# Second half of a ConvFFN: split w_up pairs kept in DRAM, the down projection as seven products

## The chip, the cores and the metric

The kernel runs on one NeuronCore of a Trainium2 chip, in one launch. The time is device microseconds of that core. Engines: PE is TensorE (matmuls; PEld is its load of the stationary operand), DVE is VectorE, ACT is ScalarE, POOL is GpSimd, SP is SyncE, from whose queue nearly all DMAs of this stage are issued, in order.

## The reference

One decoder layer, sequence 2048, width 1024, d_ff 2816, all in float32. The change touches its last part:

```python
h2 = rmsnorm(x, norm2_g) * (1 + sc2) + sh2
u = causal_dwconv(h2 @ w_up, ffn_conv_w)      # three taps, 2 x 2816 columns
u_gate, u_val = jnp.split(u, 2, axis=-1)
y = (jax.nn.silu(u_gate) * u_val) @ w_down
return x + g2 * y
```

Ahead of it stand the conditioning vector's projections, an attention and a short convolution side by side, and the output projection; they are the same in both kernels.

## The kernel before

The FFN goes through the 2048 rows in two halves of 1024 (`hv` 0 and 1): `up(0)`, `down(0)`, `up(1)`, `down(1)`.

**Splitting.** No float32 matmul is done in one pass. An operand is split into a high part (ScalarE copies it to a narrower type) and a low part (VectorE subtracts the high part from the raw tile); a product is high x high + high x low + low x high, three matmuls. `up` splits into f16 (`high`, `low`), `down` into fp32r (`split_pair`).

**up.** There are 22 column pairs `i`: 128 columns of the gate with the 128 of the value that belong to them. A pair is a 2 x 2 block product (512 of the 1024 rows of w_up by 128 columns; two blocks of 512 sequence rows) done by Strassen's and Winograd's scheme: seven products of 4 x 3 = 12 matmuls in place of eight. The sums on the side of the sequence (`b11`, `t2`, ...) are made once a half and stay in SBUF. The sums on the side of the weights (`s1` to `s4`) are made in each half anew by `up_weights`: two loads of 512 KB (L1303), two scalings on ScalarE (L1309), four sums on VectorE (L1289, L1290), splits (L1207, L1210). This is a generator, and the steps for pair i+1 are called between the products of pair i. The pairs of split weights lie in tiles `wo..0` and `wo..1`, two sets by turns. The products are gathered from PSUM by ScalarE copies and VectorE sums; then come the convolution's taps (L1391, L1396), the silu (L1405), the product y (L1408) and its store to DRAM (`y_sc`, L1409). These last steps are the generator `finish`; those of pair i are called in the time of pair i+1, and those of the last pair in `down`.

**down.** Four products per half (row block of 512 by column half of 512), each of 22 steps of 12 matmuls into four accumulators (L142). For a step, `load_pair` loads 256 KB of y and 256 KB of w_down (L1348, L1349) into a tile `raw`; `split_pair` makes `hi` (L1354) and `lo` (L1355). Each of the tags raw, hi and lo has four buffers. Loads are called up to five steps ahead, splits two. The first three steps are loaded and split in the last pair of `up` (`first_pairs`). At the end of a product `add_gated` multiplies each accumulator by the gate (L1200), adds it to x1 (L1201) and writes it out. `side` is other work called between the steps: the last `finish`, and in `down(0)` norm2 of the second half's rows and `first_weights`, which makes the weights of the second half's first pair.

**Order.** `K` keeps an instruction in the order of the program on its engine; so the order of calls is the order on the engines. An engine that waits holds all that stands behind it; a DMA queue likewise.

Of the kernel before, what the change touches and what calls it, by code (L numbers as in the profile page):

```python
# [9 lines left out]
F32 = mybir.dt.float32  # L10
# [18 lines left out]
NT = S // P  # L29
KD = D // P  # L30
NPAIR = DFF // P
EPS = 1e-6
NEG = -1.0e38
LN_PS = 9.704060527839234
# [11 lines left out]
def kernel(  # L46
# [37 lines left out]
    m_at = [dram.tile([P, S], F32, name=f"m_at{i}") for i in range(4)]  # L84
    m_cv = [dram.tile([P, S], F32, name=f"m_cv{i}") for i in range(4)]
    x1_sc = [dram.tile([P, D], F32, name=f"x1_sc{i}") for i in range(NT)]
    y_sc = [dram.tile([P, S], F32, name=f"y_sc{i}") for i in range(NPAIR)]

    ident = const.tile([P, P], F32, name="ident")
    make_identity(nc, ident)  # L90
# [1095 lines left out]
    with ExitStack() as ph:  # L1186
# [107 lines left out]
        def up_pair():  # L1294
            n, j = divmod(used[0], 4)
            used[0] += 1
            return [fb.tile([P, 1024], F16, tag=f"wo{order[2 * j + e]}{n % 2}", name="pair") for e in range(2)]

        def up_weights(i):

            raws = [raw_tile() if i else fp.tile([P, 1024], F32, tag="first", name="raw", bufs=2) for _ in range(2)]
            for raw, ct in zip(raws, (i, NPAIR + i)):
                nc.sync.dma_start(  # L1303
                    raw.rearrange("p (k n) -> p k n", n=P), w_up[:, ct * P : (ct + 1) * P].rearrange("(k p) n -> p k n", p=P)
                )
# [24 lines left out]
            low(raws[1], *pc)  # L1330
            yield

        ready = {}

        def first_weights():

# [15 lines left out]
        def split_pair(raw):  # L1352
# [3 lines left out]
            y, wd = halves((hi, lo))  # L1356
            return (*y, *wd)

        raws, pairs = {}, {}

        def first_pairs(hv):

            for i in range(3):
                raws[4 * hv, i] = load_pair(4 * hv, i)
            yield
            for i in range(3):
                pairs[4 * hv, i] = split_pair(raws.pop((4 * hv, i)))
                yield
            while True:
                yield  # L1370

        def up(hv):
# [25 lines left out]
            def finish(i, p1, Y, gate, val, yg):  # L1398

                taps(yg, gate, i)  # L1400
                add(val[:, 2:514], p1, Y)
                yield
                yv = tap(val, NPAIR + i)
                keep_halo(val, NPAIR + i)
                K(A.activation(yg, yg, AF.Silu))  # L1405
                taps(yv, val, NPAIR + i)
                yield
                K(V.tensor_tensor(yv, yg, yv, op=ALU.mult))  # L1408
                nc.sync.dma_start(y_sc[i][:, hv * 1024 : (hv + 1) * 1024], yv)  # L1409
                yield  # L1410

            wts, ops = ready.pop("wts"), ready.pop("ops")
            last = None
# [47 lines left out]
        def down(hv, side):  # L1461

            todo = [(n, i) for n in range(4 * hv, 4 * hv + 4) for i in range(NPAIR)]
# [30 lines left out]
            for _ in side:  # L1494
                pass

        steps = {Q: norm2(Q) for Q in range(4)}
        weights = first_weights()
        early = chain(steps[0], (None for _ in range(1)), steps[1], weights)
# [36 lines left out]
```

## Time and profile before

| | |
|---|---|
| median of 3 runs | 2413.41 us (2413.23 to 2414.85) |
| the profiled execution | 2413.08 us, with a span of 2411.3 |
| granted TensorE clock | 0.997 |
| TensorE busy | 2328.6 us, 97% of the span |
| VectorE busy | 1804.9 us, 75% |
| ScalarE busy | 1304.2 us, 54% |
| start of down(0) | 1516.2 us |
| start of down(1) | 2166.95 us |
| last matmul | 2406.3 us |

The durations come from the profiled execution; its span runs from the first to the last instruction, and the device time is 1.8 us longer. A window row shows how long each engine was busy in that stretch of the span, the granted clock (1.00 is full) and the DMA load. A group row gives the count, the busy time and the mean of one instruction, and the idle time ahead of the group with what ended it.

### The profile page before, as it was taken

The page shows a single profiled execution, that of the slowest core. Times are in us where ns is not written, and L with a number is a line of the kernel's source. Part 1 is how long each engine was busy: PE and PEld are TensorE (multiplying, and loading weights), DVE is VectorE, ACT ScalarE, POOL GpSimd, SP SyncE. Part 2 cuts the span into 40 slices and gives each one's busy share as a digit, 9 for nine tenths or more (in the row PEclk, how much of TensorE's full clock was granted, in tenths as well). Part 3 has the DMA queues.
Part 4 walks back from the last instruction along what each step waited for, and adds up shares of the span by engine and source line. Part 5 has one row for each costly group of instructions (what it writes and reads, how often), then busy time and mean ns, then how long its engine had stood idle before and what let it go on. Part 6 is the DMA issues. An engine that isn't in the chain of part 4 may idle for free.

```text
span 2411.3 us, 38606 instructions
## 1 busy us (share of the span) xinstructions
PE 2328.6 (97%) x14472; PEld 1403.3 (58%) x14472; DVE 1804.9 (75%) x3430; ACT 1304.2 (54%) x2136; POOL 338.5 (14%) x282
## 2 busy tenths in 40 slices
PE   5899999999999898999999999999999999999999
PEld 5764554444677675444444444788854444448887
DVE  6768885553999897366888888667878888885554
ACT  5645544320888896344565565554545565554332
POOL 0211111101777872000000000000000000000000
PEclk9999999999999999999999999999999999999999
DMA  9356685522999996353222222677632222236775
GB/s 280 133 160 169 175 249 178 155 90 81 172 190 193 190 192 168 114 172 99 88 88 88 88 88 79 227 244 222 220 126 88 88 88 88 88 105 215 230 227 183
DMA packets 428708, 368.71 MB, mean 153 GB/s; under 512 B 184208, under 2 KB 327912, under 8 KB 427496
## 3 DMA queue, kind: packets, MB, share of 16 engines
q1 hardware_dynamic: 421400, 349.40, 51.8%
q10 hardware_dynamic: 4752, 8.46, 1.0%
q0 software_dynamic: 2368, 8.39, 0.9%
q8 instruction: 113, 1.85, 0.3%
q14 instruction: 75, 0.61, 0.1%
HBM read 267.54 MB, written 65.08 MB: 138 GB/s over the span
## 4 chain that ended last, share of the span: by engine, by line
PE 85%; DVE 7%; ACT 3%; issue 2%; DMA 2%; POOL 0%; SPq 0%; DVEq 0%; ACTq 0%; POOLq 0%
PE acc L1383 33%; PE acc L142 30%; PE pr L142 10%; PE pv L142 2%; PE pt L1064 2%; PE ps L1003 1%; PE ps L1004 1%; DVE near L1071 1%; PE po L1100 1%; DVE s_t L1027 1%; PE po L1102 1%; PE po L1101 1%; ACT s_t L1044 1%; DMA far<-wide 1%; DMA raw<-in_w_down_dram 1%
## 5 line engine op out<-in xcount | busy, mean ns | idle before, releaser
L1383 PEld LDWEIGHTS <-pair 128*128 128x128 f16 x3696 | 360.9, 98 | 436.8 <-issue 0.3
L1383 PE MATMUL acc<-t,pair 128*128 128x512 f16 x2112 | 477.4, 379 | 0.0
L1383 PE MATMUL acc<-b,pair 128*128 128x512 f16 x1584 | 363.5, 379 | 0.0
L1355 DVE TENSOR_TENSOR lo<-raw,hi 128x1024 fp32r<-128x1024 f32 x176 | 211.9, 1223 | 154.7 <-ACT hi L1354 154.2
L1354 ACT ACTIVATE hi<-raw 128x1024 fp32r<-128x1024 f32 x176 | 182.4, 1055 | 178.3 <-PE acc L142 141.8
L142 PE MATMUL acc<-hi 128*128 128x512 f32 x704 | 277.0, 393 | 1.6 <-DVE t L1200 1.6
L142 PE MATMUL acc<-lo,hi 128*128 128x512 f32 x704 | 274.6, 390 | 0.6 <-DVE lo L1355 0.5
L142 PE MATMUL acc<-hi,lo 128*128 128x512 f32 x704 | 274.5, 390 | 0.0
L1396 DVE SCALAR_TENSOR_TENSOR w<-w,fcw,w 128x1024 f32<-128x1024 f32 x176 | 226.1, 1285 | 34.6 <-ACT w L1391 25.5
L142 PEld LDWEIGHTS <-h 128*128 128x128 f16 x1344 | 130.1, 98 | 97.7 <-DVE h L355 5.4
L1207 ACT ACTIVATE pair<-raw 128x1024 f16<-128x1024 f32 x132 | 138.3, 1049 | 68.5 <-DVE raw L1290 68.4
L142 PE MATMUL acc<-wp,mp 128*128 128x512 f16 x768 | 170.6, 381 | 1.1 <-DVE raw L956 1.0
L1391 ACT ACTIVATE w<-w,fcw 128x1024 f32<-128x1024 f32 x88 | 100.7, 1144 | 130.9 <-DVE w L1289 130.9
L1044 ACT ACTIVATE s_t<-s_t,nb,cst 128x2048 f32<-128x2048 f32 (+15 forms) x128 | 164.7, 1288 | 4.8
L1210 DVE TENSOR_TENSOR pair<-raw,pair 128x1024 f16<-128x1024 f32 x132 | 160.8, 1218 | 4.7 <-ACT pair L1207 4.7
L142 PEld LDWEIGHTS acc<-hi 128*128 128x128 f32 x704 | 132.2, 188 | 31.1 <-DVE t L1200 4.4
L142 PEld LDWEIGHTS acc<-lo,hi 128*128 128x128 f32 x704 | 132.3, 188 | 28.3 <-DVE lo L1355 1.6
L142 PEld LDWEIGHTS acc<-hi,lo 128*128 128x128 f32 x704 | 132.2, 188 | 27.7
L1056 POOL TENSOR_TENSOR wide<-s_t,wide 128x1024 f16<-128x1024 f32 x64 | 136.7, 2136 | 5.3
L1027 DVE CUSTOM_DVE_ANT_0 s_t<-ps,nf,mx 128x512 f32<-128x512 f32 (+1 forms) x192 | 119.5, 643 | 17.7 <-PE ps L1006 9.4
L142 PEld LDWEIGHTS <-mp 128*128 128x128 f16 x768 | 75.1, 98 | 88.7 <-issue 2.9
L142 PE MATMUL pr<-h,wh 128*128 128x512 f16 x576 | 126.5, 379 | 0.0
(344 smaller groups left out, 4184.7 us busy)
## 6 DMA issues: line engine op xcount, KB each, us to landing
raw<-in_w_up_dram SPq DMA_DIRECT2D x88, 512.0 KB, 3.8
raw<-y_sc SPq DMA_DIRECT2D x176, 256.0 KB, 4.1
raw<-in_w_down_dram SPq DMA_DIRECT2D x176, 256.0 KB, 4.4
wx<-in_w_up_dram SPq DMA_DIRECT2D x88, 256.0 KB, 3.5
y_sc<-w SPq DMA_DIRECT2D x44, 512.0 KB, 2.6
wm<-in_w_ada_dram SPq DMA_DIRECT2D x128, 128.0 KB, 3.2
wr<-in_w_in_dram SPq DMA_DIRECT2D x40, 256.0 KB, 4.5
x_t<-in_x_dram SPq DMA_DIRECT2D x16, 512.0 KB, 5.3
```

The source lines that it names most:

```text
L142: ins = T.matmul(acc, lhsT=a, rhs=b, start=st, stop=sp)
L1027: K(V.tensor_tensor_reduce(out=s_t[:, o0 + c0 : o0 + c0 + cw], in0=ps[:, 0:cw], in1=nf[:, c0 : c0 + cw], scale=1.0, scalar=-3.0e38 if g == ...
L1044: K(A.activation(cols, cols, AF.Exp, bias=nb[:, p : p + 1], scale=qk[:, 4:5], accum_out=un["l"][:, p : p + 1]))
L1056: K(G.tensor_tensor(wide[:, 1, :], s_t[:, WB * P : WU], wide[:, 0, :], op=ALU.subtract))
L1064: K(T.transpose(pt[:, b * P : (b + 1) * P], s_t[:, (b0 + b) * P : (b0 + b + 1) * P], ident))
L1207: K(A.activation(hi, raw, AF.Copy))
L1210: K(V.tensor_tensor(lo, raw, hi, op=ALU.subtract))
L1354: K(A.activation(hi, raw, AF.Copy))
L1355: K(V.tensor_tensor(lo, raw, hi.bitcast(F32), op=ALU.subtract))
L1383: K(T.matmul(acc, lhsT=a, rhs=b, start=st, stop=sp, skip_group_check=True))
L1391: K(A.activation(y, u[:, 0:1024], AF.Copy, scale=fcw[:, ct : ct + 1]))
L1396: K(V.scalar_tensor_tensor(y, u[:, m : m + 1024], fcw[:, m * 44 + ct : m * 44 + ct + 1], y, op0=ALU.mult, op1=ALU.add))
```

## The change

In the first half `up` also stores the split weights of each pair (`keep_weights`: eight DMAs, 1.84 MB). In the second half they are read back by eight loads (`kept_weights`); there are no loads of w_up, scalings, sums or splits of it there. `kept_first` takes the place of `first_weights` in the first down.

`down(0)` stays (now `down_plain`). `down(1)` is `down_seven`: the rows of the second half's two blocks, the two column halves of w_down and the two halves of each of 11 pairs of d_ff tiles make 2 x 2 blocks again, and seven products of 11 steps do the work of four of 22. Its operands are made in `up(1)`: `down_inputs` stores the pieces of y and four sums of them (`t1` to `t4`), `down_weights` loads w_down, multiplies it by the gate, makes four sums and stores all of that. Most of these stores are put off (`store_later`) to the start of the next pair (`flush`). The gate being in the weights, an eviction is one addition (`evict`); one product is evicted by ScalarE copies, and 12 additions go to POOL. Products use two sets of four accumulators by turns.

```diff
-    y_sc = [dram.tile([P, S], F32, name=f"y_sc{i}") for i in range(NPAIR)]
+    y_sc = [dram.tile([P, S // 2], F32, name=f"y_sc{i}") for i in range(NPAIR)]
+    y_op = {n: [dram.tile([P, 512], F32, name=f"y_{n}_{j}") for j in range(NJ)] for n in ("b11", "b21", "b22", "t1", "t2", "t3", "t4")}
+    w_op = {n: [dram.tile([P, D], F32, name=f"w_{n}_{j}") for j in range(NJ)] for n in ("a11s3", "a12a22", "s1s2", "s4")}
+    up_sc = [dram.tile([P, 7 * D], F16, name=f"up_sc{i}") for i in range(NPAIR)]
...
-            pa, pb, pc, pd = [up_pair() for _ in range(4)]
+            pa, pb, pc, pd = made[i] = [up_pair() for _ in range(4)]
...
+        made = {}
+        def kept_columns(pairs):
+            at = 0
+            for both in pairs:
+                for t in both:
+                    n = 512 if both is pairs[3] else D
+                    yield t[:, 0:n], slice(at, at + n)
+                    at += n
+        def keep_weights(i):
+            for t, c in kept_columns(made.pop(i)):
+                K(nc.sync.dma_start(up_sc[i][:, c], t))
+        def kept_weights(i):
+            pairs = [up_pair() for _ in range(4)]
+            for t, c in kept_columns(pairs):
+                K(nc.sync.dma_start(t, up_sc[i][:, c]))
+            yield [*halves(pairs[0]), *halves(pairs[1]), *halves(pairs[2]), halves(pairs[3])[0]]
+            while True:
+                yield
...
+        def kept_first():
+            wts = kept_weights(0)
+            ready["ops"] = next(wts)
+            ready["wts"] = wts
+            yield
...
+        def load_operands(p, j):
+            w, y = plan[p]
+            n, e = place[w]
+            raw = raw_tile()
+            K(nc.sync.dma_start(raw[:, 0:512], y_op[y][j]))
+            K(nc.sync.dma_start(raw[:, 512:1024], w_op[n][j][:, e * 512 : (e + 1) * 512]))
+            return raw
...
+        stores, sums = [], {}
+        def store_later(dst, src):
+            stores.append(lambda: K(nc.sync.dma_start(dst, src)))
+        def flush():
+            while stores:
+                stores.pop(0)()
+        def down_inputs(i, y):
+            j = i // 2
+            a, b = y[:, 0:512], y[:, 512:1024]
+            if i % 2 == 0:
+                t12 = fq.tile([P, 1024], F32, tag="lo", name="t12", bufs=4)
+                K(nc.sync.dma_start(y_op["b11"][j], a))
+                sub(t12[:, 0:512], b, a)
+                store_later(y_op["t1"][j], t12[:, 0:512])
+                sums["t12"], sums["b"] = t12, b
+                return
+            t12, b12 = sums["t12"], sums["b"]
+            t34 = fq.tile([P, 1024], F32, tag="lo", name="t34", bufs=4)
+            K(nc.sync.dma_start(y_op["b21"][j], a))
+            K(nc.sync.dma_start(y_op["b22"][j], b))
+            sub(t12[:, 512:1024], b, t12[:, 0:512])
+            sub(t34[:, 0:512], b, b12)
+            sub(t34[:, 512:1024], a, t12[:, 512:1024])
+            store_later(y_op["t2"][j], t12[:, 512:1024])
+            store_later(y_op["t3"][j], t34[:, 0:512])
+            store_later(y_op["t4"][j], t34[:, 512:1024])
+        def down_weights(j):
+            wa, wb = [fp.tile([P, 1024], F32, tag="first", name="wd", bufs=2) for _ in range(2)]
+            for e, w in enumerate((wa, wb)):
+                K(nc.sync.dma_start(w, w_down[(2 * j + e) * P : (2 * j + e + 1) * P, :]))
+            yield
+            wc, wd = [fq.tile([P, 1024], F32, tag="lo", name="wd", bufs=4) for _ in range(2)]
+            a11, a21, a12, a22 = wa[:, 0:512], wa[:, 512:1024], wb[:, 0:512], wb[:, 512:1024]
+            s1, s2, s4 = wc[:, 0:512], wc[:, 512:1024], wd[:, 0:512]
+            for w in (wa, wb):
+                K(V.tensor_tensor(w, w, gates[:, D : 2 * D], op=ALU.mult))
+                yield
+            add(s1, a21, a22)
+            sub(a21, a11, a21)
+            yield
+            sub(s2, s1, a11)
+            sub(s4, a12, s2)
+            for n, w in (("a11s3", wa), ("a12a22", wb), ("s1s2", wc)):
+                store_later(w_op[n][j], w)
+            store_later(w_op["s4"][j][:, 0:512], s4)
             while True:
                 yield
...
-                K(V.tensor_tensor(yv, yg, yv, op=ALU.mult))
-                nc.sync.dma_start(y_sc[i][:, hv * 1024 : (hv + 1) * 1024], yv)
+                if hv == 0:
+                    K(V.tensor_tensor(yv, yg, yv, op=ALU.mult))
+                    nc.sync.dma_start(y_sc[i], yv)
+                else:
+                    y = fq.tile([P, 1024], F32, tag="hi", name="y", bufs=4)
+                    K(V.tensor_tensor(y, yg, yv, op=ALU.mult))
+                    down_inputs(i, y)
                 yield
...
+                flush()
...
                 product(X, o11, "b11", True)
-                wts = up_weights(i + 1) if i + 1 < NPAIR else first_pairs(hv)
+                if i + 1 < NPAIR:
+                    wts = (kept_weights if hv else up_weights)(i + 1)
+                else:
+                    wts = first_pairs(load_operands if hv else load_pair, hv)
                 ops = next(wts)
+                if hv and i % 2:
+                    next(wsum)
...
+                if hv == 0:
+                    keep_weights(i)
+                elif i % 2:
+                    next(wsum)
+                else:
+                    wsum = down_weights(i // 2)
+                    next(wsum)
                 product(Z, os1, "t1", True)
...
+                if hv and i % 2:
+                    next(wsum)
                 add(gate[:, 514:1026], u2, Z)
...
+                if hv and i % 2:
+                    next(wsum)
                 product(Y, o22, "t4", False)
...
+        def down_seven(side):
...
+            def x1_tiles(c, n):
+                xs[c, n] = [fb.tile([P, 512], F32, tag=f"wo{4 * c + t}1", name="xs") for t in range(4)]
+                for xp, r in zip(xs[c, n], rows[c]):
+                    K(nc.sync.dma_start(xp, x1_sc[r.start // P][:, n * 512 : (n + 1) * 512]))
...
+            def gadd(o, a, b):
+                K(G.tensor_tensor(o, a, b, op=ALU.add))
+            def evict(p, t):
+                a = acc[t]
+                if p == 0:
+                    K(A.activation(u2[t], a, AF.Copy))
+                elif p == 1:
+                    add(u2[t], u2[t], a)
+                elif p == 2:
...
+                elif p == 3:
+                    add(u3[t], u2[t], a)
+                    gadd(u3[t], u3[t], xs[1, 1][t])
...
+                else:
+                    c, n = ((0, 1), (1, 0))[p - 5]
+                    add(xs[c, n][t], xs[c, n][t], a)
+                    write(c, n, t, xs[c, n][t])
+            flush()
+            extra = {(2, 2): (0, 0), (2, 6): (1, 1), (4, 3): (0, 1), (5, 2): (1, 0)}
...
+                if (p, j) == (0, 4):
+                    flush()
+                if (p, j) in extra:
+                    x1_tiles(*extra[p, j])
+                if j == 6 and p in (4, 5):
+                    c, n = ((0, 1), (1, 0))[p - 4]
+                    for t in range(4):
+                        gadd(xs[c, n][t], xs[c, n][t], u2[t])
+                if j == 0:
+                    if p in (0, 4):
...
+                    acc = sets["b" if p in (1, 3, 5) else "a"]
+                if j != NJ - 2:
+                    for t in range(4):
+                        c = slice(t * P, (t + 1) * P)
+                        for jj in (j,) if j < NJ - 1 else (j - 1, j):
+                            yh, yl, wh, wl = pairs[p, jj]
+                            for a, b, st, sp in (
+                                (yh, wh, jj == 0 and p in (0, 1, 3, 4), False), (yh, wl, False, False), (yl, wh, False, jj == NJ - 1)
+                            ):
+                                K(T.matmul(acc[t], lhsT=a[:, c], rhs=b, start=st, stop=sp, skip_group_check=True))
+                        if j == NJ - 1:
+                            evict(p, t)
...
-        for hv in range(2):
-            last = up(hv)
-            down(hv, last if hv else chain(last, steps[2], steps[3], first_weights()))
+        down_plain(chain(up(0), steps[2], steps[3], kept_first()))
+        down_seven(up(1))
```

On SyncE, from the last y store of the first half into the first down (`up_sc` are the kept weights, `raw` the tile of a step of down), the rows before are

```order
L1409 DMA y_sc_115<-w_18033 128x1024
L1348 DMA raw<-y_sc_98 128x512
L1349 DMA raw<-in_w_down_dram 128x512
L1348 DMA raw<-y_sc_99 128x512
L1349 DMA raw<-in_w_down_dram 128x512
```

and now

```order
L1514 DMA y_sc_115<-w_18344 128x1024
L1351 DMA up_sc_259<-pair 128x1024 x6
L1351 DMA up_sc_259<-pair 128x512 x2
L1383 DMA raw<-y_sc_98 128x512
L1384 DMA raw<-in_w_down_dram 128x512
```

Eight stores have come in front of the load of step 3 (`y_sc_98` is its y).

On VectorE, in the last column pair of the second half and the start of the second down, the rows before are (L1355 is the low part of a step of down, `acc` a PSUM tile, L1396 a tap; the waits are named by engine or DMA semaphore)

```order
L1289 TENSOR_TENSOR t2_23300<-t2_23222,acc_23194 128x512 [waits PE_49]
L1289 TENSOR_TENSOR w4_23230<-t2_23300,t2_23286 128x512 [waits DVE_49,Activation_49]
L1289 TENSOR_TENSOR w4_23229<-t2_23245,acc_23195 128x512 [waits DMAHW0_49,PE_49]
L1396 SCALAR_TENSOR_TENSOR w4_23316<-w4_23229,fcw_133,w4_23316 128x1024 [waits Activation_49]
L1396 SCALAR_TENSOR_TENSOR w4_23316<-w4_23229,fcw_133,w4_23316 128x1024 [waits DVE_49]
L1289 TENSOR_TENSOR w4_23230<-t2_23222,acc_23194 128x512 [waits PE_49]
L1355 TENSOR_TENSOR lo_23359<-raw_23330,hi_23358 128x1024 [waits DMAHW1_49,DMAHW0_49,Activation_49]
```

and now (`wd_23503` and `wd_23504` are two tiles of w_down, gated by L1463; `wd_23593` and `wd_23594` hold their sums; L1390 is now the low part of a step of down, L1500 a tap)

```order
L1463 TENSOR_TENSOR wd_23504<-wd_23504,gates_283 128x1024
L1293 TENSOR_TENSOR t2_23678<-t2_23596,acc_23567 128x512 [waits PE_49]
L1293 TENSOR_TENSOR w4_23604<-t2_23678,t2_23664 128x512 [waits DVE_49,Activation_49]
L1293 TENSOR_TENSOR wd_23593<-wd_23503,wd_23504 128x512 [waits PE_49]
L1294 TENSOR_TENSOR wd_23503<-wd_23503 128x512 [waits DVE_49]
L1293 TENSOR_TENSOR w4_23603<-t2_23619,acc_23568 128x512
L1294 TENSOR_TENSOR wd_23593<-wd_23593,wd_23503 128x512
L1294 TENSOR_TENSOR wd_23594<-wd_23504,wd_23593 128x512 [waits DVE_49,PE_49]
L1500 SCALAR_TENSOR_TENSOR w4_23696<-w4_23603,fcw_276,w4_23696 128x1024 [waits Activation_49]
L1500 SCALAR_TENSOR_TENSOR w4_23696<-w4_23603,fcw_276,w4_23696 128x1024 [waits DVE_49]
L1293 TENSOR_TENSOR w4_23604<-t2_23596,acc_23567 128x512
L1390 TENSOR_TENSOR lo_23754<-raw_23725,hi_23753 128x1024 [waits DMAHW1_49,DMAHW2_49,PE_49,Activation_49]
```

The low parts of steps 0 to 2 (`lo_23622` to `lo_23648` in the change) stand ahead of the sums of w_down; the sum into `wd_23593` waits for TensorE to have read `lo_23622`, which is the low part of step 0, and the one into `wd_23594` for `lo_23644`, that of step 1. The low part of step 3 (`lo_23754`) stands behind them.

On SyncE, at the same place, before (`raw_23330` is step 3 of the second down):

```order
L1409 DMA y_sc20_115<-w4_23224 128x1024 [waits DMAHW7_49,DVE_49]
L1348 DMA raw_23330<-y_sc3_98 128x512 [waits DMAHW0_49,Activation_49]
L1349 DMA raw_23330<-in_w_down_dram 128x512 [waits DMAHW1_49]
L1348 DMA raw_23333<-y_sc4_99 128x512 [waits DMAHW2_49,Activation_49]
L1349 DMA raw_23333<-in_w_down_dram 128x512 [waits DMAHW3_49]
```

and now, with two stores of y ahead of these rows (`raw_23725` is step 3):

```order
L1425 DMA w_a11s3_10_204<-wd_23503 128x1024 [waits DMAHW5_49,DVE_49]
L1425 DMA w_a12a22_10_215<-wd_23504 128x1024 [waits DMAHW6_49]
L1425 DMA w_s1s2_10_226<-wd_23593 128x1024 [waits DMAHW7_49,DVE_49]
L1425 DMA w_s4_10_237<-wd_23594 128x512 [waits DMAHW0_49,DVE_49]
L1405 DMA raw_23725<-y_b11_3_120 128x512 [waits DMAHW1_49,Activation_49]
L1406 DMA raw_23725<-w_a11s3_3_197 128x512 [waits DMAHW2_49]
```

Step 3's loads stood behind one store, of y; now they stand behind six, four of them of the gated weights and their sums, which wait for VectorE.

More of the change, by code (lines that the diff above doesn't have):

```diff
@@ L31 @@
 NPAIR = DFF // P
+NJ = NPAIR // 2
 EPS = 1e-6
@@ L1357, in split_pair @@
             return (*y, *wd)
+        plan = (("a11", "b11"), ("s2", "t2"), ("a12", "b21"), ("s3", "t3"), ("s1", "t1"), ("a22", "t4"), ("s4", "b22"))
+        place = {
+            "a11": ("a11s3", 0), "s3": ("a11s3", 1), "a12": ("a12a22", 0), "a22": ("a12a22", 1), "s1": ("s1s2", 0), "s2": ("s1s2", 1),
+            "s4": ("s4", 0),
+        }
+        def load_operands(p, j):
[5 more added lines that the diff above has]
+            return raw
@@ L1359, with first_pairs @@
         raws, pairs = {}, {}
-        def first_pairs(hv):
+        def first_pairs(load, hv):
             for i in range(3):
-                raws[4 * hv, i] = load_pair(4 * hv, i)
+                raws[0, i] = load(0, i)
             yield
             for i in range(3):
-                pairs[4 * hv, i] = split_pair(raws.pop((4 * hv, i)))
+                pairs[0, i] = split_pair(raws.pop((0, i)))
                 yield
+            while True:
+                yield
+        stores, sums = [], {}
@@ new lines, in down_weights @@
+        def down_weights(j):
[11 more added lines that the diff above has]
+            sub(a21, a11, a21)
+            yield
+            sub(s2, s1, a11)
[3 more added lines that the diff above has]
+            store_later(w_op["s4"][j][:, 0:512], s4)
@@ L1407, in finish @@
                 yield
-                K(V.tensor_tensor(yv, yg, yv, op=ALU.mult))
-                nc.sync.dma_start(y_sc[i][:, hv * 1024 : (hv + 1) * 1024], yv)
+                if hv == 0:
[5 more added lines that the diff above has]
+                    down_inputs(i, y)
                 yield
             wts, ops = ready.pop("wts"), ready.pop("ops")
-            last = None
+            last = wsum = None
             for i in range(NPAIR):
                 o11, o12, os2, os4, os3, o22, os1 = ops
+                flush()
                 X, Y, Z = [
@@ L1459, in up, with down_plain @@
             return last
-        def down(hv, side):
-            todo = [(n, i) for n in range(4 * hv, 4 * hv + 4) for i in range(NPAIR)]
+        def down_plain(side):
+            todo = [(n, i) for n in range(4) for i in range(NPAIR)]
             loaded = split = 3
```

32 lines of the change are left out of this document (added).

## The prediction

> **What bounds the kernel now.** The page's head was read first: which engine fills the span, and what the chain that ended last is made of.
>
> ```profile
> span 2411.3 us, 38606 instructions
> PE 2328.6 (97%) x14472; PEld 1403.3 (58%) x14472; DVE 1804.9 (75%) x3430; ACT 1304.2 (54%) x2136; POOL 338.5 (14%) x282
> PE 85%; DVE 7%; ACT 3%; issue 2%; DMA 2%; POOL 0%; SPq 0%; DVEq 0%; ACTq 0%; POOLq 0%
> ```
>
> TensorE is the bound over the whole, but a share of the span says nothing about one stage. So the second view is the table of windows for the stages that the change touches: in order down of the first half, up of the second, down of the second, and ten dense microseconds near the start of the first down. Columns: window, its length, busy time of PE, PEld, DVE, ACT and POOL with instruction counts, granted clock, DMA share, GB/s.
>
> ```profile
> 1520.00:1765.00 245.00, 242.77 (x1091) 198.21 (x1090) 166.88 (x206) 129.59 (x155) 0.00 (x0) 1.00 0.72 232
> 1790.00:2160.00 370.00, 370.00 (x1716) 167.44 (x1714) 329.48 (x368) 216.79 (x287) 0.00 (x0) 1.00 0.27 86
> 2168.00:2404.00 236.00, 236.00 (x1042) 195.51 (x1042) 125.46 (x116) 90.68 (x86) 0.00 (x0) 1.00 0.68 215
> 1535.00:1545.00 10.00, 10.00 (x46) 8.29 (x45) 2.45 (x2) 7.26 (x12) 0.00 (x0) 1.00 0.89 320
> ```
>
> In the second half PE is busy 370.00 of 370.00 and 236.00 of 236.00. Two things follow: taking other engines' work out of the second up can gain nothing there, and each matmul taken out of the second down is gained whole, if the rest keeps up. The third view gives the price of a matmul. The timeline shows SyncE's loads, which in steady state are paced by the products that free the buffers (columns: start, duration, engine, line, operation, tiles, count).
>
> ```profile
> 1225.77 4.84 SPq L1303 DMA_DIRECT2D raw<-in_w_up_dram  x2
> 1298.29 4.85 SPq L1303 DMA_DIRECT2D raw<-in_w_up_dram  x2
> 2191.47 0.32 SPq L1348 DMA_DIRECT2D raw<-y_sc  x1
> 2213.23 0.32 SPq L1348 DMA_DIRECT2D raw<-y_sc  x1
> ```
>
> The first two rows stand four column pairs apart: 72.52/4 = 18.13 us for a pair's 84 matmuls. The others stand eight steps of down apart: 21.76/8 = 2.72 us for 12 matmuls, 0.2267 us each.
>
> **Part 1, fewer matmuls.** The second down has 4 x 22 steps of 12 now, 1056 matmuls; seven products of 11 steps have 924. 132 x 0.2267 = 29.9 us less, the 924 keeping their form. One step still loads 512 KB per 2.72 us, as before, so the 215 GB/s stay. Its VectorE work falls (an eviction is one sum, not a product and a sum), the twelve sums on POOL each have 10 steps before someone wants them, and products alternate between two sets of accumulators. Value **-29.9**; the cover is that load rate, and it is the rate of before.
>
> **Part 2, the tail.** After the last matmul two VectorE operations follow one another; one is left.
>
> ```profile
> 2406.30 0.39 PE L142 MATMUL acc<-hi,lo 128*128 128x512 f32 x1
> 2406.72 0.69 DVE L1200 TENSOR_TENSOR t<-acc,gates 128x512 f32<-128x512 f32 x1
> 2407.45 0.69 DVE L1201 TENSOR_TENSOR xs<-xs,t 128x512 f32<-128x512 f32 x1
> ```
>
> 2407.45 - 2406.72 = 0.7: value **-0.7**.
>
> **Part 3, inside the second up.** The groups of that stage (window 1785 to 2165; busy, mean ns):
>
> ```profile
> L1210 DVE TENSOR_TENSOR pair<-raw,pair 128x1024 f16<-128x1024 f32 x62 | 75.5, 1218 | 0.0
> L1290 DVE TENSOR_TENSOR raw<-raw 128x512 f32<-128x512 f32 x40 | 27.7, 692 | 1.4
> L1408 DVE TENSOR_TENSOR w<-w,w 128x1024 f32<-128x1024 f32 x21 | 25.6, 1219 | 0.0
> L1210 DVE TENSOR_TENSOR pair<-t,pair 128x512 f16<-128x512 f32 x20 | 13.7, 684 | 0.0
> ```
>
> Per column pair VectorE loses three wide lows (3.65), a narrow one (0.68) and four sums (4 x 0.69), 7.1 us. Per two pairs it gains two gate products (2 x 1.22) and eight sums (8 x 0.69), 4.0 us a pair. It was 89% busy (329.48 of 370) and goes to about 72%. ScalarE only loses work. TensorE was full and stays full: **0**. What hides the new work is the DMA. Per two pairs it now moves 3.67 MB of kept weights in, 1.05 MB of w_down in, 1.84 MB of sums of w_down out and 1.84 MB of y out, 8.39 MB in 36.26 us: 231 GB/s, against 86. The windows show 232 GB/s at a share of 0.72 and 320 at 0.89, both with mostly reads; here 44% are writes, which no row shows at that rate. Bounds: 0, and what rival B prices. In the first half the stores of split weights add 1.84 MB per 18.13 us, from 86 to about 190 GB/s; same answer, 0.
>
> **Part 4, the start of the second down.** This is the part that the diff doesn't tell. In the last column pair of up, the rows of VectorE show the sum into `wd_23593` behind a wait on TensorE that was not there before. The tiles of `down_weights` share four buffers with the low halves of the first products: that sum must wait until step 0 of the new down is through, `wd_23594` until step 1. On SyncE the stores of these tiles stand ahead of the load of step 3. Steps 0 to 2 are loaded early; step 3 is late. Its price is built from these rows (the third is from the list of the tile raw, 1480 to 1560):
>
> ```profile
> L1354 ACT ACTIVATE hi<-raw 128x1024 fp32r<-128x1024 f32 x176 | 182.4, 1055 | 178.3 <-PE acc L142 141.8
> L1355 DVE TENSOR_TENSOR lo<-raw,hi 128x1024 fp32r<-128x1024 f32 x176 | 211.9, 1223 | 154.7 <-ACT hi L1354 154.2
> DMA to landing us min/median/max: 3.1/4.8/8.4
> L1396 DVE SCALAR_TENSOR_TENSOR w<-w,fcw,w 128x1024 f32<-128x1024 f32 x176 | 226.1, 1285 | 34.6 <-ACT w L1391 25.5
> L1391 ACT ACTIVATE w<-w,fcw 128x1024 f32<-128x1024 f32 x88 | 100.7, 1144 | 130.9 <-DVE w L1289 130.9
> L1405 ACT ACTIVATE w<-w 128x1024 f32<-128x1024 f32 x21 | 22.0, 1045 | 0.0
> ```
>
> Count from the end of up. Step 0 is done at 2.7; VectorE starts the sum at 2.9, four of 0.69 bring it to 5.7, the one that waits for step 1 is done at 6.4. SyncE then issues the last store and the two loads of step 3, the second at about 7.2. It lands 3.1 to 8.4 later, at 10.3 to 15.6; ahead of it lie up to 1.84 MB of stores, 5.7 us at 320 GB/s, so I take 13.0. Then high 1.06 and low 1.22: ready at 15.3. TensorE has finished step 2 at 8.16: 7.2 us of idle. Behind it on the same engines stand the finishing steps of the last column pair: ScalarE's tap 1.14 and silu 1.05 ahead of step 4's high, VectorE's two taps (2.57) ahead of its low. So that step is ready at 19.1 against 18.1 (1.0), and step 5, behind the y product and its sums, at 23.6 against 21.9 (1.7); after that loads run ahead. Sum 7.2 + 1.0 + 1.7 = 9.9. The bounds follow the landing: 7.2 at 10.3, 12.5 at 15.6. And 0 if the loads somehow came early (rival A). Before, TensorE went straight on at this place, so nothing is to be gained. Value **+9.9**.
>
> An idle TensorE also brings a slow clock, once in this trace; the windows' row (clock 0.59) is for the 4 us after the idle:
>
> ```profile
> 1067.90 1.12 PE L1224 MATMUL pt<-ident,w 128*128 128x128 f32 x4 [2.16 <-ACT t L1226]
> 1068.00:1072.00 4.00, 4.00 (x14) 1.96 (x15) 3.35 (x6) 3.09 (x5) 0.00 (x0) 0.59 0.44 131
> ```
>
> (4.00 us at 0.59 lose 1.6 us.) Here steps 4 and 5 wait for their operands anyway by 1.0 and 1.7, so a slow step 3 costs nothing more: 0, at most +1.7. The Trainium skill, "TensorE: Matmul & The Clock Gate", Part 1, has the clock at half after an idle window of about 3.4 us until about as long a busy one; the trace agrees in kind, its clock having dropped after 2.16 us. By that page a loss of 1.7 us is an estimate that I leave within the bound.
>
> **Part 5, the start of the first down.** Behind the last y store now stand eight stores of split weights (1.84 MB) ahead of step 3's load.
>
> ```profile
> 1508.22 0.32 SPq L1409 DMA_DIRECT2D y_sc<-w  x1
> 1508.64 0.38 SPq L1348 DMA_DIRECT2D raw<-y_sc  x1
> 1509.07 0.78 SPq L1349 DMA_DIRECT2D raw<-in_w_down_dram  x1
> 1516.20 0.58 PE L142 MATMUL acc<-hi 128*128 128x512 f32 x1
> 1532.48 1.06 ACT L1354 ACTIVATE hi<-raw 128x1024 fp32r<-128x1024 f32 x1 [3.93 <-DMA raw<-in_w_down_dram]
> ```
>
> Eight issues of 0.4 put the load at 1512.3; with 5.7 for the stores and 4.8 to land it is there at up to 1522.8, split at 1525.1. TensorE wants it at 1516.20 + 3 x 2.72 = 1524.4: 0.7 late at worst for this one, and the loads behind it inherit the queue, where ScalarE already waited 3.93 us for DMA at 1532. The first half's weights for the second up are now read ready-made, which takes two scalings and the splits out of this stage. Bounds -0.5 and +4; value **+1.5**, nearer the middle.
>
> **Sum.** 2411.3 - 29.9 - 0.7 + 0 + 9.9 + 1.5 = 2392.1 us of span. The profiled execution took 2413.08, 1.8 more than its span, and the median of the runs lies 0.3 above it: 2392.1 + 1.8 + 0.3 = **2394 us**. Its own range, with parts 4 and 5 at their bounds, is 2389 to 2401.
>
> **Rivals.** A: *the second down starts without a gap*, since the loads come early or VectorE isn't held; for it, before shows no gap there; against it, the order of SyncE's rows, which issues in order. 2394 - 9.9 = 2384.
>
> B: *the second up becomes bound by DMA*, and the change makes the kernel slower. Place: the 36.26 us of two column pairs; price: 8.39 MB at the sustained rate, eleven times. The gain of 19 us below the old time is eaten when two pairs take 38.0 us, at 221 GB/s; at 210 they take 40.0 and 11 x 3.7 = 40 us are lost: 2434. For it: 44% of the bytes are writes, and 215 to 232 GB/s already take a share of 0.68 to 0.72. Against it: 320 GB/s at 0.89, and the share per byte in the up window (0.27 at 86) belongs to smaller pieces than the kept weights are.
>
> C: *both starts cost their upper bounds*, and the slow clock adds its 1.7: 2394 + 2.6 + 2.5 + 1.7 = 2401.
>
> D: *VectorE, SyncE or the order of stores delays each column pair of the second up a little*, say 1 us each, 22 us: 2416, no faster than before. Against it: VectorE falls to 72%, and SyncE's issues of about 0.4 us are some 15 a pair, 6 us of 18.
>
> **How the numbers follow.** Forecast 0.62, A 0.13, C 0.13, B 0.08, D 0.04. Faster by over 0.2% (4.8 us, about what a measurement can tell from no change) holds for the forecast, A, C, and for a tenth of B: 0.88; with D's half and a little of B within, same is 0.03; slower 0.09. The range runs from just under A to past C: 2382 to 2406, leaving out B and D.
>
> **What would show it.** The second down should show 924 matmuls at 0.2267 us, so 209.5 us of TensorE, and about 10 us of idle in its first six steps, put down to the split of step 3 and its load; the second up still 370 of 370 at about 230 GB/s; the first down's start up to 4 us of idle. Wrong would be: a second up longer than 18.13 us a pair (B, D), no idle at the second down's start (A), or products there that wait for loads beyond the first six steps.

## The result, and the profile after

| | before | changed |
|---|---|---|
| median, first comparison | 2413.32 us (2406.97 to 2414.85, 4 runs) | 2390.1 us (2387.47 to 2394.71, 4 runs) |
| ratio | | 0.9911, 95% interval 0.9885 to 0.9936 |
| median, second comparison | 2411.87 us (2409.0 to 2414.69, 7 runs) | 2391.3 us (2390.64 to 2393.69, 4 runs), ratio 0.9915, 0.99 to 0.993 |
| span of the profiled execution | 2411.3 us | 2393.0 us |

The forecast was 2394 us, 19 less than before; 21 to 23 were measured, and 18.3 between the two profiled spans. Where they came from is read from the first and last matmuls of the stages. The list of the tile `acc` on TensorE, before (operation, count; min, median and max duration in ns, first and last start in us; `b,pair` belongs to up, `hi` and `lo` to down):

```profile
L1383 PE MATMUL acc<-b,pair x1584: 378/379/390, 1117.5 to 2164.3; 128*128 128x512 f16 x198
L142 PE MATMUL acc<-hi x704: 387/389/580, 1516.2 to 2405.8; 128*128 128x512 f32 x176
L142 PE MATMUL acc<-hi,lo x704: 387/389/401, 1516.9 to 2406.3; 128*128 128x512 f32 x176
```

and changed (L146 is the first down, L1699 the second):

```profile
L1487 PE MATMUL acc<-b,pair x1584: 379/379/390, 1119.8 to 2166.2; 128*128 128x512 f16 x198
L146 PE MATMUL acc<-hi x352: 389/389/582, 1518.5 to 1769.4; 128*128 128x512 f32 x176
L1699 PE MATMUL acc<-hi x308: 388/389/792, 2168.8 to 2388.1; 128*128 128x512 f32 x154
L1699 PE MATMUL acc<-hi,lo x308: 387/389/628, 2169.4 to 2388.5; 128*128 128x512 f32 x154
```

The changed execution is 2.3 us late already at the first matmul of the FFN (1119.8 against 1117.5), which nothing of the change touches; executions differ there. The first up is as long as before: 398.7 us in both. From there to the start of the second down it took 650.3 us (2168.8 - 1518.5) in place of 650.75 (2166.95 - 1516.2), 0.4 less. The second down takes 219.7 us to its last matmul in place of 239.4, and 4.5 us follow in place of 5.0. Sum: 2.3 - 0.4 - 19.6 - 0.5 = -18.2, against -18.3 of span. So the whole gain is in the second down, 10 us of its 30 are lost again there, and TensorE's waits from 2140 to 2390 name the place:

```profile
PE acc L1699 <- ACT hi L1389: 5.7, 1, 5.7
PE acc L1699 <- DVE lo L1390: 0.9, 2, 0.5
```

The idle time is one wait of 5.7 us and two of 0.47; the rest of the 10 us is lost to a slow clock behind them. The timeline around the long wait, the sums that VectorE was held with, SyncE's stores and the load of step 3 (L1405, L1406), and matmuls of that step, of step 4 (2189.16) and of the product's last step (2204.57):

```profile
2171.91 0.69 DVE L1293 TENSOR_TENSOR wd<-wd 128x512 f32<-128x512 f32 x1 [5.62 <-PE acc L1699]
2173.85 1.48 DVE L1294 TENSOR_TENSOR wd<-wd 128x512 f32<-128x512 f32 x2
2175.35 0.75 SPq L1425 DMA_DIRECT2D w_s<-wd  x1
2176.20 1.14 SPq L1405 DMA_DIRECT2D raw<-y_b  x1
2177.38 0.56 SPq L1406 DMA_DIRECT2D raw<-w_a11s  x1
2181.93 1.06 ACT L1389 ACTIVATE hi<-raw 128x1024 fp32r<-128x1024 f32 x1 [6.75 <-DMA raw<-w_a11s]
2183.04 0.79 PE L1699 MATMUL acc<-hi 128*128 128x512 f32 x1 [5.72 <-ACT hi L1389]
2184.30 0.79 PE L1699 MATMUL acc<-lo,hi 128*128 128x512 f32 x1 [0.47 <-DVE lo L1390]
2184.89 0.63 PE L1699 MATMUL acc<-hi,lo 128*128 128x512 f32 x1
2185.32 0.63 PE L1699 MATMUL acc<-hi 128*128 128x512 f32 x1
2189.16 0.61 PE L1699 MATMUL acc<-hi 128*128 128x512 f32 x1
2204.57 0.50 PE L1699 MATMUL acc<-lo,hi 128*128 128x512 f32 x1 [0.47 <-DVE lo L1390]
2184.16 2.60 DVE L1500 SCALAR_TENSOR_TENSOR w<-w,fcw,w 128x1024 f32<-128x1024 f32 x2
2186.68 1.22 DVE L1390 TENSOR_TENSOR lo<-raw,hi 128x1024 fp32r<-128x1024 f32 x1
2190.87 1.22 DVE L1390 TENSOR_TENSOR lo<-raw,hi 128x1024 fp32r<-128x1024 f32 x1
```

VectorE sat for 5.62 us until TensorE was through with step 0; the last store of the weights went out at 2175.35, the load of step 3 behind it at 2177.38, 8.6 us after the second down began (2168.78); it was there at 2181.9, and TensorE went on at 2183.04.

The windows answer to those of before: first down, second up, second down, the ten dense microseconds, and the six behind the gap.

```profile
1520.00:1765.00 245.00, 242.92 (x1093) 198.51 (x1093) 163.12 (x200) 123.72 (x148) 0.00 (x0) 1.00 0.71 237
1790.00:2160.00 370.00, 370.00 (x1716) 167.76 (x1715) 270.59 (x308) 107.04 (x168) 0.00 (x0) 1.00 0.66 229
2170.00:2386.00 216.00, 209.34 (x909) 172.04 (x908) 118.29 (x109) 82.98 (x81) 20.38 (x12) 0.98 0.68 229
1535.00:1545.00 10.00, 10.00 (x46) 8.28 (x45) 2.45 (x2) 5.94 (x9) 0.00 (x0) 1.00 0.99 383
2183.00:2189.00 6.00, 5.49 (x12) 4.02 (x13) 5.95 (x5) 2.92 (x3) 0.00 (x0) 0.50 0.65 229
```

The second up is full as before, with VectorE at 73% (270.59 of 370) and 229 GB/s. In the last row the granted clock is at half: from the third matmul of step 3 (2184.89) to the first of step 4 (2189.16) they start 0.427 us apart, where 0.2267 is the full rate.

### The profile page after: what moved, and what is told of

The parts are those of the page before. It is cut to its first block, busy times and chain, and to the rows that moved or that the text cites. A ratio compares the mean times of both kernels' runs of the same rounds, so it can differ in the third digit from the quotient of the medians.

```text
span 2393.0 us, 38865 instructions
## 1 busy us (share of the span) xinstructions
PE 2304.5 (96%) x14340; PEld 1385.3 (58%) x14340; DVE 1723.5 (72%) x3345; ACT 1172.7 (49%) x1997; POOL 358.6 (15%) x294
## 3 DMA queue, kind: packets, MB, share of 16 engines
q8 instruction: 112, 1.84, 0.3%
## 4 chain that ended last, share of the span: by engine, by line
PE 86%; DVE 6%; ACT 3%; DMA 2%; issue 2%; SPq 1%; POOL 0%; DVEq 0%; ACTq 0%; POOLq 0%
PE acc L1487 33%; PE acc L146 22%; PE pr L146 10%; PE acc L1699 8%; PE pv L146 3%; PE pt L1068 2%; PE ps L1007 1%; PE ps L1008 1%; DVE near L1075 1%; PE po L1104 1%; DMA far<-wide 1%; DVE s_t L1031 1%; PE po L1106 1%; PE po L1105 1%; ACT s_t L1048 1%
## 5 line engine op out<-in xcount | busy, mean ns | idle before, releaser
L1390 DVE TENSOR_TENSOR lo<-raw,hi 128x1024 fp32r<-128x1024 f32 x165 | 201.9, 1244 | 138.2 <-ACT hi L1389 135.6
L1500 DVE SCALAR_TENSOR_TENSOR w<-w,fcw,w 128x1024 f32<-128x1024 f32 x176 | 226.1, 1285 | 54.3 <-ACT w L1495 48.1
L1389 ACT ACTIVATE hi<-raw 128x1024 fp32r<-128x1024 f32 x165 | 170.4, 1054 | 166.4 <-PE acc L1699 96.2
L146 PEld LDWEIGHTS <-h 128*128 128x128 f16 x1344 | 130.2, 98 | 97.5 <-DVE h L359 5.3
L1640 POOL TENSOR_TENSOR u<-u,xs 128x512 f32<-128x512 f32 x4 | 6.0, 1531 | 1175.2 <-DMA raw<-w_s1s 1175.2
L146 PE MATMUL acc<-wp,mp 128*128 128x512 f16 x768 | 169.4, 379 | 1.1 <-DVE raw L960 1.0
L146 PE MATMUL acc<-hi 128*128 128x512 f32 x352 | 139.6, 397 | 1.6 <-DVE t L1204 1.6
L146 PE MATMUL acc<-lo,hi 128*128 128x512 f32 x352 | 137.3, 390 | 0.5 <-DVE lo L1390 0.5
L146 PE MATMUL acc<-hi,lo 128*128 128x512 f32 x352 | 137.2, 390 | 0.0
L1699 PE MATMUL acc<-hi 128*128 128x512 f32 x308 | 121.4, 394 | 5.7 <-ACT hi L1389 5.7
L146 PE MATMUL pr<-h,wh 128*128 128x512 f16 x576 | 126.5, 379 | 0.0
L146 PE MATMUL pr<-h,wl 128*128 128x512 f16 x576 | 125.8, 379 | 0.0
L146 PEld LDWEIGHTS <-mp 128*128 128x128 f16 x768 | 74.9, 98 | 87.6 <-issue 1.3
L1699 PE MATMUL acc<-lo,hi 128*128 128x512 f32 x308 | 121.1, 393 | 0.9 <-DVE lo L1390 0.9
L1699 PE MATMUL acc<-hi,lo 128*128 128x512 f32 x308 | 120.8, 392 | 0.0
```

The lines of the kernel that those rows point to most:

```text
L146: ins = T.matmul(acc, lhsT=a, rhs=b, start=st, stop=sp)
L1389: K(A.activation(hi, raw, AF.Copy))
L1390: K(V.tensor_tensor(lo, raw, hi.bitcast(F32), op=ALU.subtract))
L1500: K(V.scalar_tensor_tensor(y, u[:, m : m + 1024], fcw[:, m * 44 + ct : m * 44 + ct + 1], y, op0=ALU.mult, op1=ALU.add))
L1699: K(T.matmul(acc[t], lhsT=a[:, c], rhs=b, start=st, stop=sp, skip_group_check=True))
```

## The experiments

**Two holds in a row.** The theory: the gap has two causes, one behind the other. VectorE's sums of w_down wait for TensorE because they share buffers with the low parts of steps 0 and 1; and SyncE's load of step 3 stands behind stores that wait for those sums. The rivals: only the bytes of the stores, or only the order on SyncE, count. The change was run again and, on the same chip, with each cause taken away alone and with both.

> The changed kernel once more, beside the variants below, so that they are compared on one chip. From its first profile: 21 to 25 us faster than before; the second down takes 219.7 us from its first to its last matmul, 209.5 for 924 matmuls and 10.2 of idle and slow clock in its first ten steps. If that gap were an accident of one execution, this profile would show another one, with other waits.

Measured: 2391.3 us (2390.64 to 2393.69), ratio to before 0.9915 (0.99 to 0.993): 20.6 us faster, just short of the 21 to 25 expected. The second down took 220.9 us (2163.6 to 2384.5), with the same wait, 7.7 us long. The gap is no accident. The load of step 3, its use by ScalarE, and the wait:

```profile
2172.24 0.56 SPq L1406 DMA_DIRECT2D raw<-w_a11s  x1
2178.73 1.06 ACT L1389 ACTIVATE hi<-raw 128x1024 fp32r<-128x1024 f32 x1 [8.70 <-DMA raw<-w_a11s]
2179.84 0.80 PE L1699 MATMUL acc<-hi 128*128 128x512 f32 x1 [7.67 <-ACT hi L1389]
```

The load goes out 8.6 us after the start again, but is usable only 6.5 us later, where the first profile had 4.5. Three runs further down keep the change's order at this place (the two with added stores and the one without the read-back): there the load needs 4.3 to 5.2 us, and the second down takes 9.7 to 10.4 us over 209.5.

Other buffers for the sums:

```diff
-            wc, wd = [fq.tile([P, 1024], F32, tag="lo", name="wd", bufs=4) for _ in range(2)]
-            s1, s2, s4 = wc[:, 0:512], wc[:, 512:1024], wd[:, 0:512]
...
+            s1, s2, s4 = temp(), temp(), temp()
             add(s1, a21, a22)
...
-            for n, w in (("a11s3", wa), ("a12a22", wb), ("s1s2", wc)):
+            for n, w in (("a11s3", wa), ("a12a22", wb)):
                 store_later(w_op[n][j], w)
-            store_later(w_op["s4"][j][:, 0:512], s4)
+            for n, e, w in (("s1s2", 0, s1), ("s1s2", 1, s2), ("s4", 0, s4)):
+                store_later(w_op[n][j][:, e * 512 : (e + 1) * 512], w)
```

> The sums of w_down go into three tiles of the temporaries (tag t2) in place of two tiles of the tag lo, so that VectorE need not wait for steps 0 and 1 of the second down. SyncE's order stays: the stores of the weights still stand ahead of the load of step 3. My theory (two holds in a row: VectorE held by TensorE, then the load of step 3 held on SyncE behind the stores that wait for VectorE): the sums are through about 1 us after the end of up in place of 6.4, the load of step 3 is issued at about 2 in place of 8.6, and lands at about 6.5, just in time; but the low part of step 3 holds VectorE until 8.9, and steps 4 and 5 stay 1 and 2.5 us late. Gap of the second down about 4 in place of 10.2: 6 us faster than the change. Rival (the bytes of the stores ahead of the load make it late, whoever waits): gap still 8 or more, at most 2 us faster.

Measured: 2386.55 us (2383.94 to 2387.57), 4.7 less than the change; ratio to before 0.9892 (0.9877 to 0.9906). The second down took 215.1 us (2166.5 to 2381.6): 5.6 over 209.5, where 4 had been expected and the rival wanted 8. The timeline:

```profile
2169.39 0.56 SPq L1406 DMA_DIRECT2D raw<-w_a11s  x1
2175.31 1.06 ACT L1389 ACTIVATE hi<-raw 128x1024 fp32r<-128x1024 f32 x1 [8.14 <-DMA raw<-w_a11s]
2176.42 0.51 PE L1699 MATMUL acc<-hi 128*128 128x512 f32 x1 [1.40 <-ACT hi L1389]
2177.68 0.79 PE L1699 MATMUL acc<-lo,hi 128*128 128x512 f32 x1 [0.76 <-DVE lo L1390]
2178.27 0.63 PE L1699 MATMUL acc<-hi,lo 128*128 128x512 f32 x1
2185.53 0.50 PE L1699 MATMUL acc<-lo,hi 128*128 128x512 f32 x1 [0.72 <-DVE lo L1390]
```

VectorE is no longer held. The load goes out 2.9 us after the start in place of 8.6, but needs 5.9 us to be used, where the change's needed 4.5 in one profile and 6.5 in the other. So whether the bytes of the stores ahead of it cost something of their own is not shown: 5.9 lies within what the same load takes from one execution to the next. What the edit did change is the issue, 5.7 us earlier. The half clock appears here too: from 2178.27 to 2180.40 the matmuls of step 3 start 0.427 us apart.

The load ahead of the stores:

```diff
-            flush()
             extra = {(2, 2): (0, 0), (2, 6): (1, 1), (4, 3): (0, 1), (5, 2): (1, 0)}
...
-                if (p, j) == (0, 4):
+                if (p, j) in ((0, 0), (0, 4)):
                     flush()
```

> The tiles as in the change, but SyncE issues the loads of steps 3, 4 and 5 of the second down ahead of the stores of the weights of the last pair. My theory: step 3 is there before it is wanted, but VectorE is still held until 6.4 us after the end of up, and with it the taps and the low parts of steps 3, 4 and 5: low of step 3 at about 11 (2.5 late), step 4 about 1, step 5 about 2 late. Gap about 5.4: 5 us faster than the change. Rival (only the order on SyncE, or only the bytes of the stores, matter): the gap is gone, 10 us faster.

Measured: 2384.99 us (2384.4 to 2386.2), 6.3 less than the change; ratio 0.9889 (0.9872 to 0.9905). The second down took 214.4 us (2163.8 to 2378.2), 4.9 over; expected were 5.4. VectorE and TensorE:

```profile
2166.90 0.69 DVE L1293 TENSOR_TENSOR wd<-wd 128x512 f32<-128x512 f32 x1 [5.62 <-PE acc L1698]
2173.35 1.22 DVE L1390 TENSOR_TENSOR lo<-raw,hi 128x1024 fp32r<-128x1024 f32 x1
2174.62 0.50 PE L1698 MATMUL acc<-lo,hi 128*128 128x512 f32 x1 [2.09 <-DVE lo L1390]
2178.44 0.50 PE L1698 MATMUL acc<-lo,hi 128*128 128x512 f32 x1 [0.76 <-DVE lo L1390]
2182.64 0.50 PE L1698 MATMUL acc<-lo,hi 128*128 128x512 f32 x1 [1.16 <-DVE lo L1390]
```

The same hold of 5.62 us on VectorE; the load is early, and now the low parts of steps 3, 4 and 5 are late one after the other, each released by VectorE: 2.1, 0.8 and 1.2 us.

Both edits together:

> Both edits together: temporaries for the sums, loads of steps 3 to 5 ahead of the stores. My theory: nothing is late any more, the second down takes 209.5 to 211 us, 9 to 10 us faster than the change, about 2380 where the change has 2390. Rival (a cost that comes with the start of the second down itself, such as the clock): a gap of 3 us or more stays, and a low clock with it.

Measured: 2380.09 us (2378.27 to 2382.76), 11.2 less than the change, where 9 to 10 had been expected; ratio to before 0.9867 (0.9853 to 0.9882). The second down took 209.5 us, and the profile shows no wait of TensorE in it at all:

```profile
L1698 PE MATMUL acc<-hi x308: 389/389/578, 2162.8 to 2371.8; 128*128 128x512 f32 x154
2165.00:2370.00 205.00, 205.00 (x907) 169.78 (x905) 114.07 (x103) 81.80 (x80) 20.94 (x12) 1.00 0.69 229
```

This settles the gap: with both holds away all of it is gone, with one away about half. It is also the version that beats both kernels. The two edits nearly add up: 4.7 and 6.3 us alone, 11.2 together. So neither hold hides the other's price here; each edit alone simply leaves the other hold's half.

**What the first part of the change is worth by itself.** Its edit is the kernel before, with the stores of `keep_weights` in the first half and these two lines:

```diff
-                wts = up_weights(i + 1) if i + 1 < NPAIR else first_pairs(hv)
+                wts = (kept_weights if hv else up_weights)(i + 1) if i + 1 < NPAIR else first_pairs(hv)
...
-            down(hv, last if hv else chain(last, steps[2], steps[3], first_weights()))
+            down(hv, last if hv else chain(last, steps[2], steps[3], kept_first()))
```

> The kernel before with one part of the change: the first half stores the split pairs of w_up, the second half reads them back; the second down stays as four products of 22 steps, with no sums of y or of w_down. My theory: TensorE was already full in the second up, so that the 7 us of VectorE and 6 us of ScalarE that fall away per pair buy nothing: within 2 us of the kernel before (the start of the first down gave back 0.4 in the change's profile), second up at 18.13 us a pair. Rival (part of the change's gain comes from the relieved engines of the second up): 5 us or more faster than before.

Measured: 2411.21 us (12 runs) against 2411.29, ratio 0.9998 (0.999 to 1.0006). VectorE is busy for 189.51 of 360 us in the second up, and it buys nothing:

```profile
1790.00:2150.00 360.00, 360.00 (x1669) 163.19 (x1668) 189.51 (x199) 100.84 (x159) 0.00 (x0) 1.00 0.41 131
```

The other way round, the sums without the read-back (the second up calls `up_weights`, nothing is kept):

```diff
-                    wts = (kept_weights if hv else up_weights)(i + 1)
+                    wts = up_weights(i + 1)
...
                 if hv == 0:
-                    keep_weights(i)
+                    pass
...
-        down_plain(chain(up(0), steps[2], steps[3], kept_first()))
+        down_plain(chain(up(0), steps[2], steps[3], first_weights()))
```

> The change without its first part: the second half loads, scales, sums and splits w_up anew, and makes the sums of y and w_down besides; nothing is kept in the first half. My theory (reading back is what pays for the sums): VectorE, busy 16.1 of 18.13 us a pair before, gets 4.0 us more, 20.1, and becomes the bound of the second up: 22 x 2.0 = 43 us longer than in the change, about 2434, so 20 us slower than before although the second down still saves 30. Rival (VectorE's idle time and the slack of two pairs take it up): within 5 us of the change.

Measured: 2435.54 us (2435.02 to 2440.48), ratio 1.0097 (1.0081 to 1.0113): 24.3 us slower than before, where 20 had been expected. Two pairs take 41.0 us, 20.5 each (20.1 expected), VectorE is busy 96% of the stage, and TensorE waits for it and falls to a clock of 0.96:

```profile
1908.52 4.87 SPq L1307 DMA_DIRECT2D raw<-in_w_up_dram  x2
1949.52 4.87 SPq L1307 DMA_DIRECT2D raw<-in_w_up_dram  x2
1790.00:2150.00 360.00, 336.90 (x1486) 148.61 (x1485) 346.94 (x405) 185.99 (x247) 0.00 (x0) 0.96 0.51 166
```

From the start of the first down to that of the second it took 698.2 us (2215.2 - 1517.0) in place of 650.3. So reading back is worth nothing alone and some 44 us (2435.5 - 2391.3) as the room for the sums; the two parts can't be priced one by one.

**How far the second up is from the DMA's limit.** Half or all of a pair's split weights are stored once more in the second up:

```diff
+        def keep_again(i):
+            for e, (t, c) in enumerate(kept_columns(made.pop(i))):
+                if e < 4:
+                    K(nc.sync.dma_start(up_x[i][:, c], t))
...
                 if hv == 0:
                     keep_weights(i)
+                else:
+                    keep_again(i)
```

(`e < 8` for all of them.)

> The change, and in the second up four of the eight pieces of each pair's split weights are stored once more to a place that nobody reads: 1.05 MB a pair more, 289 GB/s in place of 231. My theory (the DMA engines have room there; they reached 383 GB/s at a share of 0.99 for ten microseconds in the first down): share 0.83, the second up still 18.13 us a pair, within 2 us of the change. Rival (the change runs at the edge of what mixed reads and writes sustain): two pairs take 45 us in place of 36.3, some 90 us more.

> As the run before, with all eight pieces stored once more: 1.84 MB a pair, 332 GB/s, share about 0.96. My theory: close to the limit; loads of the next pair's weights come late in places, 0 to 20 us more than the change. If the limit for this mix lies at 290 to 300 GB/s, two pairs take 41 us and some 50 us are lost.

Measured: 2390.71 us (2388.37 to 2394.56) and 2391.65 us (2388.79 to 2392.94), both with a ratio of 0.9914 to before (0.9899 to 0.9929, and 0.99 to 0.9929), as the change has it (0.9915). The second up of each:

```profile
1790.00:2150.00 360.00, 360.00 (x1670) 163.20 (x1668) 261.87 (x299) 99.95 (x157) 0.00 (x0) 1.00 0.82 289
```

```profile
1790.00:2150.00 360.00, 360.00 (x1669) 163.19 (x1668) 261.33 (x299) 101.52 (x158) 0.00 (x0) 1.00 0.93 332
```

At 332 GB/s, over half of it writes, TensorE is still never kept waiting. Rival B of the prediction was not near.

## Why the prediction was right, point by point

**Part 1** (-29.9): right to the tenth. With nothing in the way the second down takes 209.5 us, and before 239.4.

**Part 2** (-0.7): 0.5 in the profiles, from the last matmul to the end.

**Part 3** (0): right. The second up stayed at 18.13 us a pair, and the two experiments on its halves show why: TensorE was full with VectorE at 89%, so relief buys nothing, and the same work without relief makes VectorE the bound.

**Part 4** (+9.9): measured 10.2 and 11.4 in the two profiles of the change, by the mechanism that was read from the order. The pieces moved within it. The load of step 3 went out at 8.6 us in place of 7.2, mainly since the last store took SyncE 0.75 us and the first of the step's two issues 1.14, where the working leaves about 0.4 for each. It was usable 4.5 us later in place of the 5.8 taken. The two errors cancel, and high of step 3 began at 13.15 us (2181.93 - 2168.78) where 13.0 had been worked out. That closeness is luck: in the second profile it began at 15.1 us (2178.73 - 2163.64), still within the bounds of 10.3 to 15.6.

The 10.2 us of the first profile are 6.9 up to the second matmul of step 3 (7.2 had been worked out), 2.6 of slow clock in steps 3 and 4, and 0.6 at 2204.57, where the low part of the product's last step came late. The working had the 2.6 as waits of steps 4 and 5 (1.0 + 1.7) and did not have the 0.6. With the slow clock, step 4's low (ready at 2187.9) and step 5's (2192.1) were no longer waited for. At full clock, so these rows say, step 3 would have ended at about 2186.8, 2.5 us after 2184.30, and both would have been late, by an estimated 0.8 and 1.3 us; with the loads first, at full clock, they were late by 0.8 and 1.2. So by this estimate the clock took the place of those waits and cost a few tenths on top; no run of the change without the slow clock was made. The prediction says that the trace before has such a slow clock once. It has it in two more places: the granted clock is 0.57 in 64 to 68 us, where TensorE had idled for 3.07 us, and 0.57 in 924 to 928, behind a window of 4 us in which it did not run.

The Trainium skill, "TensorE: Matmul & The Clock Gate", Part 1, gives 426.7 ns from start to start for a matmul of 512 columns at half clock; step 3's last ten matmuls are 0.427 us apart, so the trace agrees.

**Part 5** (+1.5): the step that failed, inside its bounds. From the start of the first down to that of the second, 0.4 us were gained in place of 1.5 lost. The eight stores took SyncE 4.93 us, more than the 3.2 assumed, but the load behind them was usable at 1520.55, 3.8 us after the end of its issue:

```profile
1510.84 4.93 SPq L1351 DMA_DIRECT2D up_sc<-pair  x8
1516.32 0.46 SPq L1384 DMA_DIRECT2D raw<-in_w_down_dram  x1
1520.55 1.06 ACT L1389 ACTIVATE hi<-raw 128x1024 fp32r<-128x1024 f32 x1 [2.26 <-DMA raw<-in_w_down_dram]
1521.65 1.23 DVE L1390 TENSOR_TENSOR lo<-raw,hi 128x1024 fp32r<-128x1024 f32 x1 [0.21 <-ACT hi L1389]
```

Its low was ready at 2.3 us after that, 1522.88, and step 3 wanted it at 1518.46 + 8.16 = 1526.6. The working had put the 5.7 us of stored bytes and the full time to land one behind the other; but the stores were under way while SyncE was still issuing them: from 1510 to 1516 the DMA moved 145, 397 and 404 GB/s in three windows of 2 us, 1.9 MB of the 2.4 MB that these stores and the last store of y hold. So most of the bytes were gone when the load came. What is left of this part is small and of no steady sign: the same stretch took 650.75 us before, 650.3 in the change, 650.7 when it was run again (2163.6 - 1512.9), 650.4 to 651.5 in the five other runs that have the change's first down and its read-back, and 651.8 with the read-back alone (2166.47 - 1514.7, where VectorE's low parts held TensorE for 0.8 us in two places in place of 0.5 in one). What decides within these 1.5 us stays open.

**The rivals.** A came true only in the variant with both holds removed: 2380, where 2384 had been worked out for no gap. B is excluded by the added stores, C by part 5. D would have shown as pairs longer than 18.13 us; the second up had 1716 matmuls in 370 us before and after.

## What to carry to other kernels

When work is moved to the end of a stage, read the order of the next stage's first steps on every engine and queue: a tile that borrows a buffer from the next stage's ring waits for that stage to start, and everything behind it on its engine and on the store queue waits too. Here the load that stood behind the held stores was a second hold, and undoing either one gave back about half: when an edit leaves part of a gap, look for the second hold. And a saving on an engine that isn't the bound is worth what one puts in its place: here nothing by itself, and 44 us as room for the sums.

## What the runs showed of the hardware that was not expected

Mixed reads and writes of 332 GB/s over 360 us, at a DMA share of 0.93, delayed no load that TensorE waited for; for ten microseconds 383 GB/s were reached at 0.99.

The clock's fall did not follow the longest idle time. With other buffers for the sums TensorE idled for 1.40 and 0.76 us with a single matmul between them, and ran at half clock for about 3 us. A window from it (0.50 is the granted clock):

```profile
2178.40:2180.40 2.00, 2.00 (x6) 1.52 (x5) 1.96 (x3) 0.90 (x1) 0.00 (x0) 0.50 0.75 252
```

With the loads first it idled for 2.09 us, then for 0.76 and 1.16 with a step's matmuls between, and the clock stayed full:

```profile
2174.00:2176.00 2.00, 1.38 (x6) 1.14 (x7) 1.89 (x3) 2.00 (x3) 0.00 (x0) 1.00 0.79 259
```

What decides the clock's fall is left open; no run was made for it.
